# A mixture-of-experts decoder block: the place of the last sixteen weight loads and of the first requests

## The chip, the cores and the metric

The kernel runs on one core of one Trainium2 chip. The metric is the device time of one execution in microseconds (us), as the median of several runs. One execution was also taken by the hardware profiler; all durations below come from it. The engines are PE (matrix products; PEld is its weight load, which runs beside it), DVE (vector work), ACT (activations, copies and scaling), POOL, and SP, which here issues the DMA transfers.

## The reference

One layer of a decoder for 512 tokens of width 1024: a mixer (gated linear attention and block-sparse attention), a cross-attention into a memory, and a mixture of experts, each behind a norm and added to the residual, then a last norm. The stage that this document is about is the mixture of experts: each token goes to 2 of 32 experts, and each expert is a gated network with 512 hidden units.

```python
def hier_moe(h, w_rg, b_rg, w_re, b_re, w_gate, w_up, w_down):
    ...
    expert = grp * EXPERTS_PER_GROUP + top_i
    ...
    def run_block(args):
        e, tok, w = args
        xb = xt[tok]
        hid = jax.nn.silu(xb @ w_gate[e]) * (xb @ w_up[e])
        return (hid @ w_down[e]) * w[:, None].astype(xb.dtype)
    ...
    return out.reshape(B, S, D)
```

All weights are float32. An expert has 6 MB of them (gate and up of 1024 x 512, down of 512 x 1024), all 32 together 201 MB, and each is read once.

## The kernel before

**Stages.** The mixer, the memory attention and the routing come first, up to about 500 us. Then the experts run in 16 pairs (p = 0 to 15). Each expert has room for 64 tokens (CAP), and the two experts of a pair stand side by side in the halves of PE's output.

**One pair.** The gate and up products (gate_up, tile gu_ps) go over eight slices k of the 1024 features. Then come SiLU on ACT and the product on DVE (hidden), the transposes (hidden_t), beside them the products that add the previous pair's output to the residual (comb, tile c_ps), and for all but the last pairs the gather of tokens for the next group (gat, tiles g_ps, xT). The down products (down, tile y_ps) go over four slices ft and two halves c of the output; rows_hilo then splits y_ps into yh (ACT) and yl (DVE). Each matrix product of float32 stands in the profile as two passes.

**The weight stream.** The weights of an expert are 12 blocks of 512 KB: eight of gate and up, four of down; a pair has 24, all pairs 384. The generator load_pairs yields them in the order in which the pairs use them, gate and up of both experts slice by slice, then down. eload(n) asks until n blocks have been asked for. Asking takes a buffer from the pool bp (NB = 48 blocks, shared with xT, oh, wts and other tiles) and writes the DMA on SP; SP issues in that order, each issue held until the buffer is free and until the eighth load before it has landed, since eight semaphores take turns. Sixteen blocks are asked for in the stage before. Pair p asks for 24 p + DEPTH (30) blocks at its start, two to four more behind every second slice k, up to 46, and two more behind each slice ft of the down products, up to 54, which is how the next pairs' weights come ahead of their use.

**The spill loop.** An expert with more than 64 tokens spills into extra blocks. At the start of the last pair (p = 15) overflow reads the number of extra blocks into a register on every engine (L1266) and runs a loop over them (L1268), whose entry and exit are meetings of all five engines. Its body would load an expert's weights again and takes seven buffers of the pool. With these inputs no iteration runs. Ahead of it stands eload(24 p + SPILL_AT), 360 + 8 = 368 blocks, but the pair before has by then asked for all 384, so that this request does nothing.

**The end.** In the last pair the down products of the half c = 0 come first, then the first half of c = 1, the residual products of c = 0, and the rest (last_products, L1369 to L1375); the last norm (scale, finish) and the stores follow. SP loads gf, the gain of the last norm, behind all weights (L1327).

Of the kernel before, what the change touches and what calls it, by code (L numbers as in the profile page):

```python
# [26 lines left out]
NE = 32  # L27
# [38 lines left out]
def bcast_rows(ap, n):  # L66
    return bass.AP(tensor=ap.tensor, offset=ap.offset, ap=[[0, P], [1, n]])
# [3 lines left out]
def block_kernel(ctx, tc, x, mem, g_mem, rel_bias, g_mix, w_in, w_alpha_up, b_alpha, g_gla_head, w_proj_gla,  # L71
# [19 lines left out]
    def blk(name, shape, dt=F32):  # L91
        return bp.tile([P] + list(shape), dt, tag="b", name=name)
# [8 lines left out]
    def ps(name, shape, parts=P):  # L101
        return pp.tile([parts] + list(shape), F32, tag="p", name=name)
# [15 lines left out]
    def rows2(name, n, w=T, dt=F32):  # L118

        per = 1024 // w  # L120
        b = [blk(f"{name}{i}", [per, w], dt) for i in range(-(-n // per))]
        return [b[k // per][:, k % per, :] for k in range(n)]
# [34 lines left out]
    def drain(*gens):  # L157
        for g in gens:
            for _ in g:
                pass  # L160

    def steps(g, n):
        for _ in range(n):
            next(g, None)
# [6 lines left out]
    plan, loaded, ready, used = [], [], [], [0]  # L171
# [776 lines left out]


    blocks = [[] for _ in range(NE)]  # L950
    eloads = [0]

    def load_pairs():
        for p in range(NE // 2):
# [10 lines left out]

    def eload(n):

        while eloads[0] < min(n, 12 * NE):
            next(pair_loads)
            eloads[0] += 1  # L970

# [117 lines left out]
    drain(vgen)  # L1089
    wco.extend(wnext(2, 512) for _ in range(2))  # L1090
    eload(PRE[0])
    c_transpose(0)
    c_scores(2)
# [5 lines left out]
    for t in range(NT):  # L1099
# [8 lines left out]
        if t + 1 < NT:  # L1108
            c_values(t + 1)
        else:  # L1110
            eload(PRE[2])
            c_gather(0, [2, 3])
# [18 lines left out]
        if t == 1:  # L1131
            eload(PRE[1])
# [54 lines left out]
    def group_hots(g):  # L1187
        rel = small("rel", [NT, 2])
        V.tensor_scalar(rel, code, -float(4 * ESTR * g), None, op0=ALU.add)
        oh = blk("oh", [NT, 4 * CAP], F32R)  # L1190
        for t in range(NT):
            tile_hots(oh, rel, t, 4 * CAP)
        return oh

    def gather(oh, xT, ns):

        for k in range(KD):
            o = ps("g_ps", [ns])
            for t in range(NT):
                for q, src in enumerate((xrh, xrl)):  # L1200
                    mm(o, src[t][:, tcol(k)], oh[:, t, :], t == 0 and q == 0, t == NT - 1 and q == 1)
            S.activation(xT[k], o, AF.Copy, scale=gfeat[:, k:k + 1])
            yield

    def slot_rows(codes, n=P, oa=None):

        ot, oa = med("ot", [T], F32R)[0:n], (med("oa", [T]) if oa is None else oa)[0:n]
        c0, c1 = (cw[0][0:n, i, :] for i in range(2))
        V.tensor_scalar(oa, c0, codes, None, op0=ALU.is_equal)
        V.scalar_tensor_tensor(ot, c1, codes, oa, op0=ALU.is_equal, op1=ALU.add)  # L1210
        ws = small("ws", [2])[0:n]
        for i, c in enumerate((c0, c1)):
            V.scalar_tensor_tensor(oa, c, codes, cw[1][0:n, i, :], op0=ALU.is_equal, op1=ALU.mult,
                                   accum_out=ws[:, i:i + 1])
        V.tensor_tensor(ws[:, 0:1], ws[:, 0:1], ws[:, 1:2], op=ALU.add)
        return ot, ws


    def gate_up(gu, k, xk, ws):

        for q in range(2):
            for x, w, own in zip(xk, ws, halves):
                mm(gu[q][own], x, w[2 * (k // 2) + q][:, k % 2, :], k == 0, k == KD - 1, skip_group_check=True)

    def hidden(gu, ws, n=P, hid=None):
        hid = (med("hid", [4, P]) if hid is None else hid)[0:n]
        row = hid.rearrange("p a b -> p (a b)")
        S.activation(row, gu[0][0:n], AF.Silu)  # L1228
        V.scalar_tensor_tensor(row, row, ws[:, 0:1], gu[1][0:n], op0=ALU.mult, op1=ALU.mult)  # L1229
        return hid  # L1230

    def hidden_t(hid, n=P):
        t_ps = ps("ht_ps", [4, n])
        for a in range(4):
            PE.transpose(t_ps[:, a, :], hid[:, a, :], ident[0:n, 0:n])  # L1235
        hid_t = med("hid_t", [4, n])
        S.activation(hid_t, t_ps, AF.Copy)
        return hid_t

    def down(y_ps, hid_t, ft, ws, cs=(0, 1)):  # L1240
        for c in cs:
            for i, (w, own) in enumerate(zip(ws, halves)):
                mm(y_ps[c][own], hid_t[:, ft, 64 * i:64 * i + 64], w[8 + ft][:, 512 * c:512 * c + 512], ft == 0,
                   ft == 3, skip_group_check=True)

    def rows_hilo(y, n=P, parts=None):
        parts = [a[0:n] for a in parts or (med("yh", [512], F32R), med("yl", [512], F32R))]
        split(*parts, y[0:n])
        return parts
# [5 lines left out]
    def combine(ot, ys):  # L1255

        for t in range(NT):
            for c, y in ys.items():
                o = ps("c_ps", [512])
                product(o, ot, t, y)  # L1260
                xs = x_sb[t][:, 512 * c:512 * c + 512]
                V.tensor_tensor(xs, o, xs, op=ALU.add)  # L1262
                yield t, c
# [38 lines left out]
    for p in range(NP):  # L1302
        w = blocks[2 * p:2 * p + 2]
        used = 24 * p
        if p == NP - 1:
            eload(used + SPILL_AT)
            overflow(*spilled)
        eload(used + DEPTH)
        if p % 2 == 0 and p:
            xT = xT_next  # L1310
        gu = [ps("gu_ps", [512]) for q in range(2)]
        s0 = (p % 2) * P
        for k in range(KD):
            gate_up(gu, k, [xT[k][:, s0 + CAP * i:s0 + CAP * i + CAP] for i in range(2)], w)
            if k % 2:
                eload(used + DEPTH + 2 * (k + 1))
            if p == 0 and k >= BC_AT:
                next(bcast, None)
                if k == BC_AT + 3:
                    slot = slot_rows(sid[:, 0:1])  # L1320
                    oh_next = group_hots(1)
        if p % 2 == 0 and p + 2 < NP:
            xT_next = rows2("xT", KD, 4 * CAP)
            gat = gather(oh_next, xT_next, 4 * CAP)
        if p == NP - 1:
            gf = blk("gf", [D])
            SY.dma_start(gf, bcast_rows(g_final, D))  # L1327
        hid = hidden(gu, slot[1])
        gs = 4 if p + 2 < NP else 0
        steps(gat, min(gs, 1))  # L1330
        steps(comb, 2 if gs else 4)
        hid_t = hidden_t(hid)
        for i in range(3):
            steps(gat, min(gs, 1))
            steps(comb, 2)
        drain(comb)
        ot = slot[0]
        if p + 1 < NP:
            slot = slot_rows(sid[:, 2 * p + 2:2 * p + 3])
        if p % 2 and p + 3 < NP:  # L1340
            oh_next = group_hots((p + 3) // 2)
        if p >= 2:
            next(spill, None)
        y_ps = [ps("y_ps", [512]) for c in range(2)]
        if p == NP - 1:
            break
        for ft in range(4):
            down(y_ps, hid_t, ft, w)
            eload(used + DEPTH + 16 + 2 * (ft + 1))
        ys = {c: rows_hilo(y_ps[c]) for c in range(2)}  # L1350
        comb = combine(ot, ys)
# [59 lines left out]
SPILL_AT = 8  # L1411
# [6 lines left out]
NB = 48  # L1418
WARM = (14, 12)
DEPTH = 30  # L1420
AHEAD, SAHEAD = 4, 2
FILL = (4, 3), (5, 3), (5, 4), (5, 4)
MANUAL = None
# [28 lines left out]
```

## Time and profile before

| what | value |
|---|---|
| median of three runs | 1001.63 us (1000.63 to 1001.95) |
| the profiled execution's own time | 1001.05 us |
| its span, first to last instruction | 999.2 us |
| PE busy | 959.1 us (96%) |
| DVE busy | 475.5 us (48%) |
| ACT busy | 311.8 us (31%) |
| bytes moved | 252.52 MB, mean 253 GB/s |

A row of the order of time reads: start in us, duration in us, engine, source line, operation, output <- input, shapes, count (x), and in brackets how long the engine stood idle before it and what ended that. "SPq" is SP's queue issuing a DMA; "PEq" is PE's sequencer. A row of the list of waits reads: who waited, at which line, for whom, the total in us, how often, and the longest. A row of the DMA issues has the number of issues, KB of each, and the median us from issue to landing. A row on a source line has engine and operation, the count, the shortest, median and longest duration in ns, and when the first and last began.

### The profile page before, as it was taken

The numbers are of one execution on the slowest core, as the hardware profiler recorded it, in microseconds if no ns is written. First come the engines' busy times: TensorE is split into PE (matmuls) and PEld (weight loads), VectorE is DVE, ScalarE is ACT, GpSimd is POOL, SyncE is SP. The second block draws the span as 40 slices with busy tenths as digits, with TensorE's granted clock in tenths as the row PEclk, the third lists the DMA queues.
The fourth block names the chain that finished last, engine by engine and source line by source line (L and its number), as shares of the span: only waits on it lengthen the run. The fifth ranks groups of instructions, "written<-read, shape, count | busy, mean of one in ns | idle before, by whom it ended". The sixth has DMA issues, their size and how long they took to land. (4 is left out here: it accounts for less than half of the span.)

```text
span 999.2 us, 13897 instructions
## 1 busy us (share of the span) xinstructions
PE 959.1 (96%) x5305; PEld 642.0 (64%) x5305; DVE 475.5 (48%) x1048; ACT 311.8 (31%) x631; POOL 33.4 (3%) x46
## 2 busy tenths in 40 slices
PE   9999999999999999999999999999999999999475
PEld 7889779887888888898844455555444555543122
DVE  6343863445556845467741445444243545322305
ACT  5442643455546434455331111111111111110003
POOL 3200010000000000000000000000000000000003
PEclk9999999999999999999999999999999999999878
DMA  9512346222143505383689999999999999999942
GB/s 300 153 43 64 66 71 181 57 70 85 64 163 130 195 19 146 115 296 126 253 316 376 410 409 409 409 408 409 410 409 409 410 408 409 409 409 410 409 190 85
DMA packets 117161, 252.52 MB, mean 253 GB/s; under 512 B 10310, under 2 KB 61795, under 8 KB 117092
## 3 DMA queue, kind: packets, MB, share of 16 engines
q1 hardware_dynamic: 117092, 251.60, 68.6%
q8 instruction: 43, 0.70, 0.3%
q14 instruction: 26, 0.21, 0.1%
HBM read 247.90 MB, written 3.67 MB: 252 GB/s over the span
## 5 line engine op out<-in xcount | busy, mean ns | idle before, releaser
L136 PE MATMUL gu_ps<-we,xT 128*64 128x512 f32 x1024 | 228.1, 598 | 22.5 <-PEq L1268 21.2
L136 PEld LDWEIGHTS gu_ps<-we,xT 128*64 128x64 f32 x1024 | 75.3, 138 | 169.3 <-issue 157.4
L213 DVE TENSOR_TENSOR wlo<-wraw,whi 128x1024 fp32r<-128x1024 f32 (+1 forms) x71 | 86.4, 1236 | 90.1 <-ACT whi L212 89.8
L136 PE MATMUL y_ps<-we,hid_t 128*64 128x512 f32 x512 | 113.6, 595 | 0.3 <-issue 0.3
L1229 DVE SCALAR_TENSOR_TENSOR hid<-hid,ws,gu_ps 128x512 f32<-128x512 f32 x16 | 12.0, 747 | 211.1 <-PE gu_ps L136 211.1
L1262 DVE TENSOR_TENSOR x<-c_ps,x 128x512 f32<-128x512 f32 x120 | 76.7, 685 | 38.9 <-PE c_ps L136 38.9
L131 PE MATMUL fo<-hTh,whi 128*128 128x512 f32 x224 | 90.5, 404 | 0.0
L133 PE MATMUL fo<-hTh,wlo 128*128 128x512 f32 x224 | 87.5, 391 | 0.0
L132 PE MATMUL fo<-hTl,whi 128*128 128x512 f32 x224 | 87.4, 390 | 0.0
L136 PEld LDWEIGHTS y_ps<-we,hid_t 128*64 128x64 f32 x512 | 35.7, 137 | 68.9 <-issue 58.1
L1228 ACT ACTIVATE hid<-gu_ps 128x512 f32<-128x512 f32 x16 | 9.6, 597 | 213.7 <-PE gu_ps L136 213.7
L212 ACT ACTIVATE whi<-wraw 128x1024 fp32r<-128x1024 f32 (+2 forms) x73 | 74.5, 1043 | 2.0 <-DMA wraw<-in_w_in_dram 1.9
L136 PE MATMUL g_ps<-oh,xrh 128*128 128x256 f32 x256 | 64.6, 293 | 1.7 <-DVE oh L1030 1.7
L136 PE MATMUL g_ps<-oh,xrl 128*128 128x256 f32 x256 | 61.6, 281 | 0.0
L136 PEld LDWEIGHTS g_ps<-oh,xrh 128*128 128x128 f32 x256 | 47.0, 189 | 14.9 <-PE gu_ps L136 9.7
L133 PE MATMUL ro<-whi,hTl 128*128 128x256 f32 (+1 forms) x192 | 55.3, 288 | 0.8 <-DVE hTl L333 0.8
L132 PE MATMUL ro<-wlo,hTh 128*128 128x256 f32 (+1 forms) x192 | 55.3, 288 | 0.7 <-POOL wlo L213 0.7
L131 PE MATMUL ro<-whi,hTh 128*128 128x256 f32 (+1 forms) x192 | 55.8, 291 | 0.0
L212 ACT ACTIVATE yh<-y_ps 128x512 fp32r<-128x512 f32 x32 | 19.1, 598 | 109.3 <-PE y_ps L136 109.3
L136 PE MATMUL c_ps<-yh,ot 128*128 128x512 f32 x128 | 50.7, 396 | 0.7 <-ACT yh L212 0.7
L136 PE MATMUL c_ps<-yl,ot 128*128 128x512 f32 x128 | 50.7, 396 | 0.2 <-DVE yl L213 0.2
L131 PEld LDWEIGHTS fo<-hTh,whi 128*128 128x128 f32 x224 | 42.0, 188 | 12.0 <-issue 3.9
(320 smaller groups left out, 1545.7 us busy)
## 6 DMA issues: line engine op xcount, KB each, us to landing
we<-in_w_exp_gate_dram SPq DMA_DIRECT2D x128, 512.0 KB, 10.2
we<-in_w_exp_up_dram SPq DMA_DIRECT2D x128, 512.0 KB, 10.2
we<-in_w_exp_down_dram SPq DMA_DIRECT2D x128, 512.0 KB, 10.2
wraw<-in_w_in_dram SPq DMA_DIRECT2D x38, 512.0 KB, 3.9
wraw<-in_w_out_dram SPq DMA_DIRECT2D x8, 512.0 KB, 4.5
wraw<-in_w_ckv_dram SPq DMA_DIRECT2D x8, 512.0 KB, 4.6
wraw<-in_w_proj_gla_dram SPq DMA_DIRECT2D x4, 512.0 KB, 3.9
wraw<-in_w_proj_moba_dram SPq DMA_DIRECT2D x4, 512.0 KB, 4.2
```

Of the source, the lines that this page charges most:

```text
L131: PE.matmul(o, lh, rh, start=first, stop=False)
L132: PE.matmul(o, lh, rl, start=False, stop=False)
L133: PE.matmul(o, ll, rh, start=False, stop=last)
L136: PE.matmul(o, l, r, start=first, stop=last, **kw)
L212: S.activation(hi, src, AF.Copy)
L213: eng.tensor_tensor(lo, src, f(hi), op=ALU.subtract)
L1228: S.activation(row, gu[0][0:n], AF.Silu)
L1229: V.scalar_tensor_tensor(row, row, ws[:, 0:1], gu[1][0:n], op0=ALU.mult, op1=ALU.mult)
L1262: V.tensor_tensor(xs, o, xs, op=ALU.add)
```

## The change

Two things. First, eload gets a ceiling that starts at 12 x 30 + 8 = 368 blocks; the ceiling is raised to 384 only behind overflow. Second, the first pair asks by a table of its own: 34 blocks at its start instead of 30, and 37, 41, 44 and 47 behind the slices k = 1, 3, 5, 7 instead of 34, 38, 42 and 46. The requests behind its down products (48 to 54), and all those of the other pairs below the ceiling, are as before.

```diff
-    eloads = [0]
+    eloads, elimit = [0], [12 * (NE - 2) + SPILL_AT]
...
-        while eloads[0] < min(n, 12 * NE):
+        while eloads[0] < min(n, elimit[0]):
...
         if p == NP - 1:
-            eload(used + SPILL_AT)
+            eload(elimit[0])
             overflow(*spilled)
-        eload(used + DEPTH)
+            elimit[0] = 12 * NE
+        eload(used + D0[0] if p == 0 else used + DEPTH)
...
             if k % 2:
-                eload(used + DEPTH + 2 * (k + 1))
+                eload(D0[1 + k // 2] if p == 0 else used + DEPTH + 2 * (k + 1))
...
+D0 = 34, 37, 41, 44, 47
```

SP at the entry of the spill loop, before: the numbers in the names are those of the buffers, and we_8063 is load 384.

```order
L946 DMA we_8001<-in_w_exp_down_dram 128x1024
L946 DMA we_8003<-in_w_exp_down_dram 128x1024
L946 DMA we_8061<-in_w_exp_down_dram 128x1024
L946 DMA we_8063<-in_w_exp_down_dram 128x1024
L1266 TENSOR_LOAD rt_xi_6457
L1268 COMPARE_AND_BRANCH
L1268 UNCONDITIONAL_BRANCH
```

SP at the same place in the change; we_7951 is load 368.

```order
L940 DMA we_7927<-in_w_exp_gate_dram 128x1024
L940 DMA we_7929<-in_w_exp_up_dram 128x1024
L940 DMA we_7949<-in_w_exp_gate_dram 128x1024
L940 DMA we_7951<-in_w_exp_up_dram 128x1024
L1266 TENSOR_LOAD rt_xi_6457
L1268 COMPARE_AND_BRANCH
L1268 UNCONDITIONAL_BRANCH
```

Loads 369 to 384 have gone from ahead of the count's read. Behind the loop's last branch SP now has them, from we_8276 on; before, the load of gf stood there at once.

```order
L1268 UNCONDITIONAL_BRANCH
L940 DMA we_8276<-in_w_exp_gate_dram 128x1024
L940 DMA we_8278<-in_w_exp_up_dram 128x1024
L940 DMA we_8280<-in_w_exp_gate_dram 128x1024
L940 DMA we_8282<-in_w_exp_up_dram 128x1024
L940 DMA we_8284<-in_w_exp_gate_dram 128x1024
L940 DMA we_8286<-in_w_exp_up_dram 128x1024
L940 DMA we_8288<-in_w_exp_gate_dram 128x1024
L940 DMA we_8290<-in_w_exp_up_dram 128x1024
L946 DMA we_8292<-in_w_exp_down_dram 128x1024
L946 DMA we_8294<-in_w_exp_down_dram 128x1024
```

Six more loads of down weights follow, and then gf. On PE, DVE, ACT and POOL no instruction changes its place.

In the first pair SP's loads keep their order and place; a buffer's number shows how early it was asked for. From load 38 (we_5047) to load 44, as a difference:

```order
 L940 DMA we_5047<-in_w_exp_up_dram 128x1024
-L940 DMA we_5069<-in_w_exp_gate_dram 128x1024
-L940 DMA we_5071<-in_w_exp_up_dram 128x1024
-L946 DMA we_5073<-in_w_exp_down_dram 128x1024
+L940 DMA we_5049<-in_w_exp_gate_dram 128x1024
+L940 DMA we_5051<-in_w_exp_up_dram 128x1024
+L946 DMA we_5053<-in_w_exp_down_dram 128x1024
 L946 DMA we_5075<-in_w_exp_down_dram 128x1024
-L946 DMA we_5114<-in_w_exp_down_dram 128x1024
-L946 DMA we_5116<-in_w_exp_down_dram 128x1024
+L946 DMA we_5077<-in_w_exp_down_dram 128x1024
+L946 DMA we_5079<-in_w_exp_down_dram 128x1024
```

Loads 39 to 41 and 43 to 44 are asked for one step earlier; 38 and 42 are not moved against the other tiles.

## The prediction, made before the change was run

> **What bounds the kernel now.** I read the page's forty slices first, then the table of stretches for the rate of the weight stream.
>
> ```profile
> span 999.2 us, 13897 instructions
> PE   9999999999999999999999999999999999999475
> PEclk9999999999999999999999999999999999999878
> DMA  9512346222143505383689999999999999999942
> 525.00:550.00 25.00, 25.00 (x132) 11.91 (x129) 5.37 (x9) 3.82 (x7) 0.00 (x0) 1.00 1.00 383
> 600.00:900.00 300.00, 299.62 (x1540) 146.95 (x1536) 125.28 (x252) 46.01 (x86) 0.00 (x0) 1.00 1.03 409
> we<-in_w_exp_down_dram SPq DMA_DIRECT2D x128, 512.0 KB, 10.2
> ```
>
> The columns of a stretch are its bounds and length, the busy time of PE, PEld, DVE, ACT and POOL, the granted clock, the DMA share and GB/s. From about 525 us on, PE and DMA are both full: the 384 expert blocks come at 409 GB/s, so 512 KB take 1.28 us, and a block lands 10.2 us after its issue, that is with eight blocks in flight. The one hole is PE's slice 38 (a 4, near 940), while DMA still shows 9. The list of waits and the order of time on SP and PE tell what it is (SP's rows come from two windows).
>
> ```profile
> PE gu_ps L136 <- PEq L1268: 21.2, 1, 21.2
> 930.80 0.33 SPq L940 DMA_DIRECT2D we<-in_w_exp_up_dram  x1
> 932.88 0.33 SPq L940 DMA_DIRECT2D we<-in_w_exp_gate_dram  x1
> 941.85 0.33 SPq L940 DMA_DIRECT2D we<-in_w_exp_up_dram  x1
> 952.09 0.33 SPq L946 DMA_DIRECT2D we<-in_w_exp_down_dram  x1
> 955.70 0.33 SPq L1327 DMA_DIRECT2D gf<-in_g_final_dram  x1
> 929.79 4.89 PE L136 MATMUL y_ps<-we,hid_t 128*64 128x512 f32 x22
> 955.84 16.02 PE L136 MATMUL gu_ps<-we,xT 128*64 128x512 f32 x64 [21.15 <-PEq L1268]
> 976.12 5.37 PE L136 MATMUL y_ps<-we,hid_t 128*64 128x512 f32 x24
> 979.85 0.60 ACT L212 ACTIVATE yh<-y_ps 128x512 fp32r<-128x512 f32 x1 [4.82 <-PE y_ps L136]
> ```
>
> PE ends the down products of pair 14 at 934.68 and stands until 955.84 in front of the spill loop of line 1268. SP has to issue all of its loads up to number 384 (952.09; load 368 is the row at 930.80, load 376 the one at 941.85) before it gets to that loop, one each 1.28 us. No iteration runs: the down rows count 128 blocks, 32 experts by four. So the loop costs nothing but a meeting of all engines, and the last engine to come is SP, for the sake of the weight queue. The two sources of the loop show the meeting:
>
> ```profile
> L1266 DVEq TENSOR_LOAD <-rt_xi x1: 544/544/544, 935.5 to 935.5; - x1
> L1266 SPq TENSOR_LOAD <-rt_xi x1: 486/486/486, 952.5 to 952.5; - x1
> L1268 SPq EVENT_SEMAPHORE  x28: 17/17/17, 953.0 to 955.6; - x28
> L1268 DVEq EVENT_SEMAPHORE  x8: 21/21/21, 936.2 to 955.6; - x8
> L1268 POOLq EVENT_SEMAPHORE  x4: 17/17/17, 953.8 to 955.5; - x4
> ```
>
> SP reads the count at 952.5, POOL answers at 953.8, and PE runs at 955.84: 2.04 us from POOL's answer. DVE had been there since 935.5.
>
> **The change, part by part.** *Ceiling.* It takes nothing away and adds no instruction: SP's 16 issues 369 to 384 (8.4 MB) move behind the loop, with their waits, past the loop's meeting, ahead of the load of gf. While SP waits for the other engines there, only these loads and gf stand behind it, and PE waits for them. What is gained first is PE's wait. SP reaches the loop after load 368: 930.80 + 0.33, and its own 1.39 us from the end of its last issue to POOL's answer (953.8 - 952.42), so 932.5. Then DVE is last, with its read at 935.5 and first event at 936.2. I add 0.2 us for its own events and the 2.04 us: PE would go on at **938.4**, SP at 938.3 (gf stands 0.14 us ahead of PE). Bounds: 938.2, and 938.8 if DVE's read to PE's start took the 3.3 us that SP's takes (952.5 to 955.84). PE alone would be 17.4 us earlier.
>
> What is late next is the weights. The last load of the gate and up products of pair 15 is number 376, the last of all 384. If the stream does not notice SP's pause, they land 10.2 us after 941.85 and 952.09: 952.05 and 962.3. For the end of the stream the stretches have:
>
> ```profile
> 956.00:958.00 2.00, 2.00 (x6) 0.66 (x7) 0.00 (x0) 0.00 (x0) 0.00 (x0) 0.50 1.04 412
> 962.00:964.00 2.00, 2.00 (x12) 0.66 (x10) 0.00 (x0) 0.00 (x0) 0.00 (x0) 1.00 0.16 64
> 964.00:966.00 2.00, 2.00 (x12) 0.73 (x10) 0.00 (x0) 0.00 (x0) 0.00 (x0) 1.00 0.00 0
> ```
>
> After 962 some 128 KB move, mostly of gf, which was issued last; so load 384 lands between 962.3 and 962.8, and I take 962.5.
>
> Does the stream notice? Before, load 369 is issued at 932.88 and lands by 943.1. After, it is issued at 938.3, 5.4 us later, when of eight blocks in flight some three are left (load 368, issued at 930.80, lands at 941.0). The nearest row for a load into a short queue is that of other 512 KB loads:
>
> ```profile
> wraw<-in_w_in_dram SPq DMA_DIRECT2D x38, 512.0 KB, 3.9
> 503.00 0.33 SPq L940 DMA_DIRECT2D we<-in_w_exp_gate_dram  x1
> 503.43 0.38 SPq L940 DMA_DIRECT2D we<-in_w_exp_up_dram  x1
> 503.90 0.38 SPq L940 DMA_DIRECT2D we<-in_w_exp_gate_dram  x1
> ```
>
> So load 369 lands at 942.2, still ahead of 943.1, and issues can follow every 0.45 us: load 376 is out at 938.3 + 7 x 0.45 = 941.5, where it was before (941.85). The pause costs 0; its bounds are 0 and 5.4 us, the whole of SP's delay, if each us without an issue were lost to the stream.
>
> Now pair 15, from rows of before. A pass of the down products takes 0.215 us (the 32 of a whole pair and the 24 here differ by 8; 5.37 = 24 x 0.215 + 0.2). Gate and up products are 64 passes, four blocks per 16 passes: 3.44 us of PE for 5.12 us of DMA, so PE waits for each block. Behind load 376 ten passes are left: 952.05 + 2.15 + 0.2 = 954.4. From the end of these products (971.86) to the down products (976.12) there are 4.26 us: 958.7. The down products of the first half take each pair of blocks as it lands; the last two of their 16 passes need load 384. In the profile these two start at 976.12 + 14 x 0.215 = 979.13, and yh follows 0.72 us later (979.85). With load 384 at 962.5, yh starts at 963.2; by PE alone it would be 958.7 + 3.73 = 962.4. From yh to the end nothing is changed, and gf, ordered right behind load 384, lands by 964 and is wanted by the products after yh, 3.2 us behind it (xg). So the gain is 979.85 - 963.2 = **16.6 us**; the bounds are 17.4 (PE alone) and 16.6 - 5.4 = 11.2 (pause wholly exposed). If the cover of eight blocks in flight were gone, the latter would be the price.
>
> *First pair.* Loads 31 to 47 are asked for at an earlier place of the first pair, one to four at a time. SP's issues stay in the same order; what moves is which buffer a load, or wts, oh and xT of the next pair, takes from the pool of 48. SP around there:
>
> ```profile
> 507.19 0.33 SPq L940 DMA_DIRECT2D we<-in_w_exp_gate_dram  x1
> 508.03 0.33 SPq L940 DMA_DIRECT2D we<-in_w_exp_up_dram  x1
> 508.45 16.51 SPq L946 DMA_DIRECT2D we<-in_w_exp_down_dram  x8
> 525.05 0.38 SPq L940 DMA_DIRECT2D we<-in_w_exp_gate_dram  x1
> SPq L946 <- PE y_ps L136: 7.1, 1, 7.1
> SPq L946 <- PE gu_ps L136: 6.2, 3, 3.2
> ```
>
> These issues end with a PE product that frees a buffer. A load with an older buffer goes one group of products earlier, 0.84 us (508.03 - 507.19). But load 48 waits 7.1 us for the first down products, and from there (525) the stream is full to the end. Pair 0 uses none of loads 31 to 47. So what comes earlier ahead of load 48 is waited out there: 0, with bounds of 0.84 us gained, if the stream's start moved by one group, and 0.84 lost, if a buffer of oh or xT came one group later and PE passed it on.
>
> *Sum.* 1001.05 us is the profiled execution's own time (span 999.2, and 1.85 around it); 1001.05 - 16.6 - 0 = 984.45. The median of the three runs, 1001.63, is 0.58 above it, so I forecast 985.0 for the median.
>
> **The rivals.** *The pause shows (16%).* The stream loses part or all of the 5.4 us: up to 985.0 + 5.4 = 990.4. For it: eight blocks are all that is in flight, and SP is stopped for more than half of their 10.2 us. Against: the estimate for load 369, 0.9 us ahead of its old landing.
>
> *SP is late behind the loop (4%).* Its next instructions come after a taken branch; if they had to be brought in through the full DMA queues, the first issue could come as late as a block's 10.2 us behind 938.3. Then load 384 lands at 948.5 + 3.9 + 15 x 1.28 = 971.6, yh starts at 972.3, the gain is 7.5 and the time 994.1. Against: gf went out 0.1 us after SP's last event (955.6 to 955.70), through the same branch. [...]
>
> *The ceiling does nothing (1%).* If PE's wait were for something other than SP, it would stay 21.2 us, and the time 1001.6. Against: PE goes on 3.3 us behind SP's read, whereas the other engines stand there from 936.
>
> *More than that (4%).* The stream starts one group earlier and the landing is at 962.3: 985.0 - 0.84 - 0.2 = 984.0, or, with PE alone as the limit, 984.2.
>
> *Slower (2%).* One mechanism: SP leaves the loop later than it does now. With 16 loads behind it, load 384 lands 3.9 + 15 x 1.28 = 23.1 us after SP's first issue and yh starts 0.7 later, so from an issue at 956.0 on the kernel is slower, 1 us for each us. Two fetches of 10.2 us one after the other, instead of the one above, would bring the issue to 958.7 and the time to 1001.6 + 2.7 = 1004.3. Against: the loop is now left with the stream running until 964.
>
> **How the numbers follow.** The forecast, 985.0 within 984.2 to 986.5, has 73%. The range reaches down to 983.8 and up to 988.5, which takes in most of the first rival; about 2 in 10 stay outside, nearly all above. About 0.2% is what a measurement of this kernel can tell from no change; faster by more than that has 97%, the same 1%, slower 2%.
>
> **What would show it.** In the profile after: PEq L1268 holds PE some 3.7 us instead of 21.2; SP issues 368 at 930.8 and the next at 938.3; between them the DMA share stays near 1.0; pair 15's gate and up products start at 938.4 and stretch to 954.4 with small waits for weights; yh at 963.2; the first pairs' rows stay where they are. The prediction is wrong if the DMA share dips behind 938, if the first issue behind the loop comes well after 938.3, or if stage one moves by more than 0.8 us.

## The result, and the profile after

The changed kernel takes **985.06 us** (median of 4 runs, 984.58 to 986.19), the kernel before 1001.13 us (4 runs, 1000.16 to 1001.95): a ratio of 0.9841, 95% interval 0.9824 to 0.9859. The profiled execution took 985.10 us, with a span of 983.3. Between two executions the stages ahead of the experts drift by up to 1.6 us (the first gate and up product of pair 0 comes at 499.89 in the changed kernel and at 501.50 with the ceiling alone), so positions in the last pair are read below as distances within one execution.

SP's and PE's rows in the order of time, around the last two pairs of the changed kernel (start, duration, engine, line, operation, tiles, count, idle before and its releaser):

```profile
931.21 0.33 SPq L940 DMA_DIRECT2D we<-in_w_exp_up_dram  x1
938.72 0.33 SPq L940 DMA_DIRECT2D we<-in_w_exp_gate_dram  x1
943.25 0.42 SPq L940 DMA_DIRECT2D we<-in_w_exp_up_dram  x1
953.87 0.33 SPq L1328 DMA_DIRECT2D gf<-in_g_final_dram  x1
928.01 7.09 PE L136 MATMUL y_ps<-we,hid_t 128*64 128x512 f32 x32
938.86 16.50 PE L136 MATMUL gu_ps<-we,xT 128*64 128x512 f32 x64 [3.77 <-PEq L1268]
959.63 5.98 PE L136 MATMUL y_ps<-we,hid_t 128*64 128x512 f32 x24
963.92 0.60 ACT L212 ACTIVATE yh<-y_ps 128x512 fp32r<-128x512 f32 x1 [5.38 <-PE y_ps L136]
```

PE's wait at the loop is 3.77 us where it was 21.15. SP's last load ahead of the loop is the first row, the first behind it the second, 7.5 us later; the eighth behind it (load 376, third row) is out at 943.25, 12.04 us behind load 368, where it was 11.05 behind it before (941.85 - 930.80). The products of pair 15 stretch, 16.50 us for 64 passes, where 64 x 0.215 + 0.2 would be 13.96. Little of that is waiting for weights. By 938.86 some blocks of the pair had landed, and PE ran on them for 12 us without such a wait. For about 3.4 of these 12 us its granted clock was 0.50 (the rows are in the last section); by an estimate from that, half the time, 1.7 us, was lost. The waits for weights come only at the end. These are PE's weight loads there, with the idle time before them:

```profile
951.29 0.19 PEld L136 LDWEIGHTS gu_ps<-we,xT 128*64 128x64 f32 x3 [0.28 <-DMA we<-in_w_exp_gate_dram]
952.57 0.20 PEld L136 LDWEIGHTS gu_ps<-we,xT 128*64 128x64 f32 x4 [0.70 <-DMA we<-in_w_exp_up_dram]
962.81 1.48 PEld L136 LDWEIGHTS y_ps<-we,hid_t 128*64 128x64 f32 x9 [0.42 <-DMA we<-in_w_exp_down_dram]
```

Without a wait the idle time between two such loads is 0.26 to 0.29 us at full clock, so that the first of these rows is no real wait. The down products then wait for weights as well (third row): yh begins 4.29 us behind the first of them, against 3.73 us before, when all weights had landed.

The meeting at the loop, read from the loop's two source lines (count, durations in ns, when the first and the last began):

```profile
L1266 SPq TENSOR_LOAD <-rt_xi x1: 485/485/485, 931.6 to 931.6; - x1
L1266 DVEq TENSOR_LOAD <-rt_xi x1: 545/545/545, 936.0 to 936.0; - x1
L1268 POOLq EVENT_SEMAPHORE  x4: 17/17/17, 936.8 to 938.5; - x4
```

SP now reads the count at 931.6 and DVE, at 936.0, is the last to come. POOL answers at 936.8, and PE starts 2.06 us later.

The weight stream in stretches of the changed kernel (bounds, length, busy time of PE, PEld, DVE, ACT, POOL, granted clock, DMA share, GB/s), then the same end of the stream before:

```profile
934.00:938.00 4.00, 1.09 (x6) 0.14 (x2) 1.38 (x2) 1.20 (x2) 0.00 (x0) 1.00 0.92 369
938.00:942.00 4.00, 3.14 (x10) 1.18 (x12) 0.00 (x0) 0.00 (x0) 0.00 (x0) 0.73 0.87 312
942.00:946.00 4.00, 4.00 (x18) 1.63 (x16) 0.00 (x0) 0.00 (x0) 0.00 (x0) 0.84 1.02 378
958.00:960.00 2.00, 2.00 (x10) 1.25 (x10) 2.00 (x5) 0.54 (x1) 0.00 (x0) 1.00 1.02 408
960.00:962.00 2.00, 2.00 (x12) 0.71 (x9) 0.99 (x2) 0.00 (x0) 0.00 (x0) 1.00 1.04 414
962.00:964.00 2.00, 2.00 (x10) 0.90 (x9) 0.00 (x0) 0.07 (x1) 0.00 (x0) 1.00 0.24 88
964.00:966.00 2.00, 2.00 (x9) 0.81 (x6) 0.69 (x1) 0.52 (x1) 0.00 (x0) 1.00 0.00 0
```

```profile
934.00:938.00 4.00, 0.68 (x4) 0.00 (x0) 1.38 (x2) 1.09 (x2) 0.00 (x0) 1.00 1.03 410
958.00:960.00 2.00, 2.00 (x6) 0.53 (x4) 0.00 (x0) 0.00 (x0) 0.00 (x0) 0.50 0.85 291
960.00:962.00 2.00, 2.00 (x12) 0.77 (x10) 0.00 (x0) 0.00 (x0) 0.00 (x0) 0.99 0.56 225
```

SP's pause can be seen: against 410 GB/s the three stretches from 934 to 946 lack 4 x (41 + 98 + 32) = 684 KB, 1.7 us of the stream. The end has not moved: in both kernels the stream is over between 962 and 964. Before, it tapered off from 958 on (291, 225, 64 GB/s, that is 1160 KB); after, it runs full until 962 (408, 414, 88, that is 1820 KB). The 660 KB more at the end are the ones missing in the pause. My reading is that not all DMA engines had been needed to the end, and that those which used to finish early paid for the pause. The profile has only the mean share of the engines (0.85, 0.56 and 0.16 in the last three stretches before), so this is not shown engine by engine; but the run without the loop, which has no pause, tapers off in the same way (373, 266 and 98 GB/s from 958 to 964).

### The profile page after: what moved, and what is told of

It is laid out like the page before. It is cut to its first block, busy times and chain, and to the rows that moved or that the text cites. A ratio compares the mean times of both kernels' runs of the same rounds, so it can differ in the third digit from the quotient of the medians.

```text
span 983.3 us, 13899 instructions
## 1 busy us (share of the span) xinstructions
PE 961.1 (98%) x5305; PEld 645.5 (66%) x5305; DVE 474.8 (48%) x1048; ACT 311.7 (32%) x631; POOL 32.7 (3%) x46
## 5 line engine op out<-in xcount | busy, mean ns | idle before, releaser
L136 PEld LDWEIGHTS gu_ps<-we,xT 128*64 128x64 f32 x1024 | 78.0, 138 | 150.5 <-issue 134.6
## 6 DMA issues: line engine op xcount, KB each, us to landing
we<-in_w_exp_gate_dram SPq DMA_DIRECT2D x128, 512.0 KB, 10.2
we<-in_w_exp_up_dram SPq DMA_DIRECT2D x128, 512.0 KB, 10.2
we<-in_w_exp_down_dram SPq DMA_DIRECT2D x128, 512.0 KB, 10.2
```

The costliest lines, as they stand in the source:

```text
L136: PE.matmul(o, l, r, start=first, stop=last, **kw)
```

## The experiments

For each run two distances are given, within its one profiled execution: E, from the first gate and up product of pair 0 to the first yh of the last pair, and L, from the down products of pair 14 to that yh. Before, E is 979.85 - 500.19 = 479.66 and L 52.25; after, E is 963.92 - 499.89 = 464.03 and L 35.91 us.

**The ceiling alone** (first pair as before; the edit is against the changed kernel):

```diff
-        eload(used + D0[0] if p == 0 else used + DEPTH)
+        eload(used + DEPTH)
-                eload(D0[1 + k // 2] if p == 0 else used + DEPTH + 2 * (k + 1))
+                eload(used + DEPTH + 2 * (k + 1))
```

> Only the ceiling of 368; the first pair asks as before. Main theory (the whole gain is PE's wait at the spill loop): 985.0 us, within 0.8 of the changed kernel; PEq at the loop holds PE 3.8 us, yh of the last pair begins at 963 to 964, load 49 issues at 524.8 to 525.1. Rival (the first pair's table gives part of the gain, at most the 0.84 us of one product group): 985.9.

Measured: 985.68 us (984.39 to 986.47), ratio to before 0.9843 (0.9827 to 0.9860); E 463.77, L 35.91. PE goes on 10.85 us behind the start of pair 14's down products, as in the changed kernel (3.76 us of wait). This execution was 1.6 us later at the first pair, which is why yh stands at 965.27. The times alone can't tell 985.0 from the rival's 985.9, but L is the same and E no longer than with the table: the whole gain is there without it.

**The first pair alone** (the other half of the diff, on the kernel before).

> Only the first pair's table; no ceiling. Main theory: no difference, 1001.1 us, PE's wait at the loop stays 21 us, load 49 issues where it did (525.05, within 0.4). Rival (the table moves the stream's start by one product group): 1000.3, and load 49 at 524.2 or earlier.

Measured: 1001.37 us (10 runs), against 1001.31 of before; ratio 1.0002 (0.9993 to 1.0012). E 479.39. SP's and PE's rows, and SP's waits between 498 and 530, of this run:

```profile
507.07 0.33 SPq L940 DMA_DIRECT2D we<-in_w_exp_gate_dram  x1
507.50 0.38 SPq L940 DMA_DIRECT2D we<-in_w_exp_up_dram  x1
524.95 0.38 SPq L940 DMA_DIRECT2D we<-in_w_exp_gate_dram  x1
SPq L946 <- PE y_ps L136: 7.1, 1, 7.1
956.00 15.49 PE L136 MATMUL gu_ps<-we,xT 128*64 128x512 f32 x64 [21.52 <-PEq L1268]
```

The table does what it says: load 40 follows load 39 by 0.43 us instead of 0.84. But load 48 waits its 7.1 us as before, and load 49 goes out at 524.95 (525.05 before), in both runs 24.86 us behind the first gate and up product of pair 0. It is worth nothing here.

**No spill loop** (on the kernel before; tokens beyond an expert's 64 would be left out):

```diff
             eload(used + SPILL_AT)
-            overflow(*spilled)
```

> The kernel of before without the spill loop (tokens beyond an expert's 64 would be left out; with these inputs there are none). Main theory (after the change the loop costs nothing more, the weight stream sets the end): 985.0 us, yh of the last pair at 963 to 964, PE goes from pair 14 to pair 15 without a wait at a sequencer, and no dip of the DMA share near 938. Rival (the pause in SP's issues still costs the 5.4 us by which load 369 is late): 979.6, yh near 958.5. Rival (PE's wait of 21 us was not for SP): 1001.

Measured: 985.61 us (985.32 to 985.98), ratio 0.9847 (0.9830 to 0.9863); E 463.24, L 35.81. PE and the stream of this run:

```profile
935.39 5.08 PE L136 MATMUL gu_ps<-we,xT 128*64 128x512 f32 x18
941.51 1.08 PE L136 MATMUL gu_ps<-we,xT 128*64 128x512 f32 x4 [1.04 <-DMA we<-in_w_exp_gate_dram]
942.79 2.79 PE L136 MATMUL gu_ps<-we,xT 128*64 128x512 f32 x12 [0.20 <-DMA we<-in_w_exp_up_dram]
960.08 5.88 PE L136 MATMUL y_ps<-we,hid_t 128*64 128x512 f32 x24
938.00:942.00 4.00, 2.96 (x16) 0.77 (x12) 0.00 (x0) 0.00 (x0) 0.00 (x0) 1.00 1.03 410
```

PE starts pair 15 at once (6.92 us behind the start of pair 14's down products, against 10.85), no stretch dips, and the kernel is no faster. PE waits 1.04 and 0.20 us for weights, again and again, and its gate and up products end 27.35 us behind the start of pair 14's down products, as they do in the changed kernel (938.86 + 16.50 - 928.01). So the changed kernel has back all that the loop cost, and the stream sets the end.

**Other ceilings**: SPILL_AT = 0, 4, 12 and 16 in place of 8, with the first pair's table kept.

```diff
-SPILL_AT = 8
+SPILL_AT = 4
```

> Ceiling 360 by SPILL_AT = 0, the first pair's table kept: all 24 loads of the last pair behind the loop. Main theory: the queue has run dry (load 360 lands near 931), PE still goes on at 938.4 to 938.9, but load 361 lands at 942.2 instead of 932.9, so the stream ends 9.3 us later: 994.3 us. Rival (a pause is always hidden): 985.0.

> Ceiling 364 in place of 368 by SPILL_AT = 4 with the first pair's table kept: twenty loads behind the loop. Main theory (the queue of eight blocks covers a pause until a load issued at 938.3 would have had to land): load 365 lands at 942.2 instead of 938.0, the stream ends 4.2 us later, 989.2 us. Rival (a pause is always hidden): 985.0. Rival (each us without an issue beyond 1.28 is lost): 985.0 + 11.3 = 996.3.

> Ceiling 372 by SPILL_AT = 12, the first pair's table kept: twelve loads behind the loop. Main theory: SP comes last to the loop, near 938.9, PE goes on near 941, 2.1 us later than in the changed kernel; PE then sets the end: yh near 964.6 to 965.5, 986.3 us, and the DMA share shows no dip. Rival (only the pause in the stream matters, PE has room): 984.5 or less.

> Ceiling 376 by SPILL_AT = 16, the first pair's table kept: eight loads behind the loop. Main theory: SP is last, its loads hold it 8 x 1.28 = 10.2 us longer than 368 does; PE goes on near 945.8 to 946.3, 10.0 us earlier than before, and is the limit: 991.3 us; PE's wait at the loop is 11 us. Rival (the loop waits for landings, not for SP): 1001.

Each ratio is to executions of the kernel before that were taken along with the run (medians 1001.13 to 1001.96).

| loads ahead of the loop | us (runs) | ratio to before (95%) | L, us | expected us |
|---|---|---|---|---|
| 360 | 996.29 (3) | 0.9943 (0.9926 to 0.9960) | 46.17 | 994.3 |
| 364 | 991.44 (2) | 0.9905 (0.9885 to 0.9925) | 43.43 | 989.2 |
| 368 (the change) | 985.06 (4) | 0.9841 (0.9824 to 0.9859) | 35.91 | |
| 372 | 986.49 (4) | 0.9844 (0.9826 to 0.9863) | 36.43 | 986.3 |
| 376 | 990.93 (2) | 0.9892 (0.9869 to 0.9916) | 42.64 | 991.3 |
| 384 (before) | 1001.13 (4) | 1 | 52.25 | |

Two limits cross at 368 to 372. Above 368, PE waits for SP: the wait at the loop is 3.8, 5.4, 11.0 and 21.2 us for 368 (where DVE is the last to come), 372, 376 and 384. The last two steps are 10.2 us for 8 loads and 5.6 for 4, 1.3 to 1.4 us for each load, as the theory has it; up to 372 most of the step is hidden, since SP comes last there by only a little (it reads the count at 938.2, DVE at 937.1). With 372 the time was met more closely than the steps: PE goes on 1.6 us later than in the changed kernel, not 2.1, and yh in L 0.5 us later, where 964.6 at the least would have been 0.7 (964.6 - 963.92). In time alone 372 can't be told from 368, since the intervals overlap. That PE sets the end there, as forecast, is seen in its down products, which take 5.37 us without a wait for weights. Below, the stream starves. SP, POOL and four stretches of the run with 364, in that order:

```profile
925.14 0.33 SPq L940 DMA_DIRECT2D we<-in_w_exp_up_dram  x1
937.78 0.33 SPq L940 DMA_DIRECT2D we<-in_w_exp_gate_dram  x1
L1268 POOLq EVENT_SEMAPHORE  x4: 17/17/17, 935.9 to 937.6; - x4
934.00:938.00 4.00, 0.23 (x4) 0.12 (x4) 1.38 (x2) 0.60 (x1) 0.00 (x0) 0.94 0.10 35
938.00:942.00 4.00, 4.00 (x12) 1.31 (x14) 0.00 (x0) 0.00 (x0) 0.00 (x0) 0.64 0.68 221
942.00:946.00 4.00, 1.88 (x8) 0.43 (x4) 0.00 (x0) 0.00 (x0) 0.00 (x0) 1.00 0.86 299
946.00:950.00 4.00, 3.69 (x12) 1.13 (x14) 0.00 (x0) 0.00 (x0) 0.00 (x0) 0.72 1.02 418
```

The eight blocks in flight are gone after some 10 us of a pause of 12.6 (925.14 to 937.78). My expectations for 360 and 364 were too low, by 2.0 and 2.2 us in time, and in L by 1.0 and 3.3 us: L should have grown by 9.3 and 4.2 over the changed kernel, and grew by 10.26 and 7.52. They counted the pause alone and let the stream go on at its full rate; but in the 8 us behind the restart it moves 221 and 299 GB/s. From 938 to 946 the run with 364 lacks 4 x (189 + 111) = 1200 KB, 2.9 us, of the order of the 3.3 us that were missed. Why it comes back so slowly, and why 364 lost more by it than 360, was not tried.

**One buffer more** (49 weight buffers; the pool of small tiles gives up two of 13 for it), and its control with 11 small buffers alone:

```diff
-NB = 48
+NB = 49
-MB = 13
+MB = 11
```

> The changed kernel with 49 weight buffers instead of 48, paid for with 11 instead of 13 of the small tiles' buffers. What bounds the changed kernel by the main theory is the weight stream, and its start is held by load 48, which waits 7.1 us for a buffer that the first down products free. With one buffer more one load more is out before them: the stream ends one block, 1.28 us, earlier, 983.8 us. Rival (the stream has no effect left on the end, PE sets it): 985.0. Rival (11 small buffers hold DVE or PE up): above 985.5.

> The changed kernel with 11 instead of 13 buffers for small tiles alone, as the control of the run with 49: 985.0 us if these two buffers are not needed, more if they are.

Measured: 983.76 us (5 runs, 983.29 to 985.20), ratio to before 0.9822 (0.9809 to 0.9836); E 461.92. The control, one execution: 986.40 us, E 463.68, beside 464.03 of the change and 463.77 of the ceiling alone, so the two small buffers are not missed from the first pair on. Its time, 1.3 us above the change, came with a late start (first gate and up product at 501.49); what one execution leaves open is whether the stages before lose by them. With 49 and the same 11 it is at 500.57, and the ceiling alone, with 13, had 501.50. SP and its waits in the run with 49:

```profile
507.98 9.92 SPq L946 DMA_DIRECT2D we<-in_w_exp_down_dram  x8
525.02 0.33 SPq L940 DMA_DIRECT2D we<-in_w_exp_gate_dram  x1
SPq L940 <- PE y_ps L136: 8.8, 3, 7.1
```

All eight down loads of pair 1 are out by 517.9, where the last of them had waited for the first down products; now it is the next load (a gate block) that waits the 7.1 us. E is 1.76 us shorter than in the control, somewhat more than one block time of 1.28, and the stream is early by as much: load 368 goes out 429.18 us behind the first gate and up product, 431.00 in the control. This version is the fastest seen; its interval and that of the change overlap, so that the step from 985.06 to 983.76 rests on E and on SP's rows rather than on the times.

## Why the prediction was right

- *Where the time was.* PE's 21.2 us were for SP, and SP was late by its loads. The runs with other ceilings show it: above 368 the wait follows the number of loads ahead of the loop.
- *PE's restart.* Forecast 10.8 us behind the start of pair 14's down products (938.4 - 927.60), measured 10.85. DVE is the last to come, as forecast.
- *What is late next.* The weights, not PE: shown by the run without the loop, in which PE starts 3.9 us sooner and nothing is gained. But PE is close behind them: at yh it has only some 0.6 us to spare (4.29 against 3.73). One step on the way there was wrong, that PE waits for each block. It does so without the loop; in the changed kernel it starts behind landed blocks, runs through them, and meets the stream only at load 376, which sets the end of these products all the same.
- *The pause is covered.* It costs some 0.1 us (L 35.91 against 35.81 without a loop, one profiled execution each; the other three with 368 and a loop have 35.89 to 35.94). The forecast had the time of it right and the profile of it wrong: it expected the DMA share to stay near 1.0 and named a dip behind 938 as a mark of failure. The share fell to 0.87, and what was lost came back at the end, where the stream used to taper off. So the zero came out, but for another reason than the forecast gave, and to that extent by luck. That load 369 would land ahead of its old time, 0.9 us, was an estimate of one load; the burst behind it ran below full rate, and load 376 went out later against load 368 by 1 us, not at the same time.
- *The size.* The sum gave 16.6 us; the medians differ by 16.07, the profiled executions by 15.95, and L by 16.34. Of the 0.7 us between the sum and the profiled executions, 0.4 is that this execution reached pair 14 later (928.01 against 927.60), and 0.3 is in L. The last wait of PE's weight loads for down weights ends at 962.81, 34.8 us behind the start of pair 14's down products, where the forecast had load 384 (962.5 - 927.60 = 34.9); but yh follows 1.1 us later, not 0.7. The gate and up products end 27.35 us behind that start, not 26.8: the last passes take 2.79 us (the row at 953.03 without the loop), not ten times 0.215 and 0.2. That did not count, since yh waits for weights that come later. That 985.0 met 985.06 so closely is luck: the forecast added 0.58 us for the median of before, 1001.63, which over four runs is 1001.13, and its gain is 0.5 us too large; the two cancel.
- *The first pair.* Nothing, as forecast, and for the reason given: load 48 waits for the down products whatever comes before it.
- *The rivals.* The late first issue behind the loop did not come: SP's load followed POOL's last event by 0.2 us (938.5 to 938.72). In the changed kernel three packets of the kind "instruction" moved between 938.6 and 941 and none from then to 960, and SP's third issue, at 939.63, took 1.56 us where the seven others up to 943.25 took 0.33 to 0.45; the profile does not tell whether it waited for them. The 10.2 us that this rival counts there once, and the slower case twice, were the author's estimate from a block's time; no run shows a delay of that size, and what was measured in its place is the 0.2 us.

## What to carry to other kernels

A loop that never ran held PE up for 21.2 us here, since its entry is a meeting of all engines and one of them had a long queue of work ahead of it in program order; look for who comes last, and move work that nobody waits for yet behind the meeting. How much to move has two sides: the queue that is interrupted must still have enough in flight to cover the pause, here eight blocks of 1.28 us against 7.5 us, and a queue that had run dry lost more than the late restart alone (7.5 us of L with 364, where 4.2 had been counted). Requests made earlier were worth nothing (a ratio of 1.0002), since a later one still waited its 7.1 us for the same buffers; one buffer more was worth 1.8 us of E.

## What the runs showed of the hardware

A stream of 512 KB loads that had run dry did not come back at its rate at once: with 364 loads ahead of the loop it moved 221 and then 299 GB/s from 938 to 946, and 418 only after that, from 946 to 950. With 360 it moved 304 from 942 to 946 and 419 after that.

PE's granted clock fell although PE had gone on. In the changed kernel PE stood for 3.77 us, ran from 938.86, and had half its clock from about 939.9 to 943.3:

```profile
938.00:939.00 1.00, 0.14 (x2) 0.17 (x4) 0.00 (x0) 0.00 (x0) 0.00 (x0) 1.00 0.66 266
939.00:940.00 1.00, 1.00 (x6) 0.41 (x6) 0.00 (x0) 0.00 (x0) 0.00 (x0) 0.93 0.97 303
941.00:942.00 1.00, 1.00 (x4) 0.30 (x2) 0.00 (x0) 0.00 (x0) 0.00 (x0) 0.50 1.02 410
943.00:944.00 1.00, 1.00 (x6) 0.47 (x4) 0.00 (x0) 0.00 (x0) 0.00 (x0) 0.86 0.99 373
```

Why it fell then, no run shows. With 364 loads ahead of the loop PE stood for the same 3.77 us and ran from 937.91; there the clock was 0.64 from 938 to 942 and 1.00 from 942 to 946.

The lower clock cost at most 0.1 us at the end (L 35.91 against 35.81 without the loop), though PE was not waiting for weights at that time: it used up time that PE would have waited later. The run without the loop had a clock of 1.00 in every stretch from 930 to 976 and took as long. With the ceiling alone the gate and up products took still longer, 16.86 us against 16.50, and L is 35.91 us all the same.
